# One filler job moved from the mLSTM heads to the attention, a third partial sum begun in the last head, and one weight sum fetched early in a hybrid mLSTM and sparse attention block

## The chip, the cores and the metric

The kernel runs on one core of one Trainium2 chip. The metric is device time in microseconds (us), lower is better: 615.52 us for the kernel before, the median of three runs (615.37, 615.52 and 616.9).

## The reference, cut to what matters

One decoder layer on 512 tokens of width 1024, in float32:

```
hN = rmsnorm(x, norm_g)
p  = split(hN @ w_in)                       # q, k, v, gates ... of both branches
mh = head_layernorm(mlstm(conv(q), conv(k), v, i, f))        # 4 heads of 256
ya = sigmoid(o) * mh * silu(z)
yb = nsa(...) * silu(z')                    # 8 heads of 64: compressed, selected, window
merged = sigmoid(g_a) * (ya @ w_branch_a) + sigmoid(g_b) * (yb @ w_branch_b)
x = x + merged @ w_out
out = rmsnorm(x, final_norm_g)
```

## The kernel before, in words

**Products.** Each float32 operand is split into a high part and a low rest (`split`, line 143: ScalarE or another engine rounds the high part, VectorE subtracts), and each block of a product is three matmuls: high by high, high by low, low by high. Weights come by `weights` (line 154): a DMA on SyncE's queue into a raw tile `wr`, then `wh` by ScalarE and `wl` by VectorE. Each of these three has three buffers, so a new DMA waits until VectorE has finished the split three loads back, and a new split waits until TensorE has finished the job three back.

**Filler.** Projections, gates and branch products are jobs of a queue, `Stream` (line 174). The attention and the mLSTM heads call `stream.step(n)` between their own matmuls; each step issues one filler matmul, and with no job left it issues nothing (lines 189 to 191). Loads run two jobs ahead. A gate job (`gate_ab`, line 575) is 24 matmuls of 512 columns, a tanh, and a store of its 256 KB to DRAM (`away`); there are sixteen, eight of `GB` and eight of `GA`, the latter in the order `in_turn` = 0, 4, 1, 5, 2, 6, 3, 7. Ten of them are queued before the attention (lines 782 to 797), six in the mLSTM's part (lines 1413 to 1416).

**Attention.** Sixteen units (line 1059). A unit computes the scores of the next unit, one call of `tick` (4 steps) after each of four, then transposes its own scaled probabilities `P` in four groups, again with a `tick` after each, and multiplies them with the values. The scaling of `P` by the reciprocal sum and the gate is four GpSimd operations behind the last score of a unit (lines 966 to 973). The last unit has no next one, so its scaling lies directly ahead of its own transposes. When the last head pair is collected, the path `zpath(3)` is added, 24 matmuls more.

**mLSTM heads.** Four heads, with 90 steps each: 24 between the scores, 24 between the value products, `NORM_FILL` = 30 behind the norm's small operations, and 6 behind each of the two groups of transposes that write `ya`. The queue there holds four convolution jobs, the gate jobs, eight jobs of branch B of 12 matmuls, and `first_of_a` (line 1396): the first six of eight blocks of branch A for two column groups, 18 matmuls each, which need only heads 0 to 2. Their sums stay open in PSUM, one in the bank `PO`, one in one of the three banks `PP`.

**Merge and end.** After the heads, `branch_a` (line 1541) finishes the eight column groups in the order `in_turn`: 6 matmuls where a sum is begun, 24 where none is. Behind each, VectorE multiplies with the gate `g`, adds branch B's part `b`, and splits the result; after each second group it forms four sums for the last product (`sums`, line 1529). That last product, by `w_out`, is done with seven half-size products in place of eight (a Strassen-Winograd scheme): four sums of blocks of `w_out` are made in DRAM by accumulating DMAs, in the chores of the heads (lines 1038 to 1049 and 1464), and loaded as weights. Each product is two jobs of 12 matmuls. The fourth sum is loaded by `load4` (line 1727) in two halves through `wr`, and split into the tiles `T4h` and `T4l` (`p4`). The last lines (`third`, `fourth`, `gen4`) form the final output rows, their norm and their stores, with the orders of ScalarE and VectorE fixed as written from `gen3` on (line 1751).

**Order.** The build orders each engine's instructions by their place in the program and by its own estimate of when their inputs are there; each engine then runs its list in order. Where the list has an instruction whose input is late, what stands behind it waits.

Of the kernel before, what the change touches and what calls it, by code (L numbers as in the profile page):

```python
# [11 lines left out]
F32 = mybir.dt.float32  # L12
F32R = mybir.dt.float32r
# [5 lines left out]
T = 512  # L19
# [57 lines left out]
def build(  # L77
# [3 lines left out]
    nc = tc.nc  # L81
# [24 lines left out]
    wp = ctx.enter_context(tc.tile_pool(name="wp", bufs=2))  # L106
    psum = ctx.enter_context(tc.tile_pool(name="psum", bufs=2, space=bass.MemoryType.PSUM))

    def bank(tag, bufs):
        return psum.tile([128, 512], F32, name=tag, tag=tag, bufs=bufs)  # L110

    PP = lambda: bank("pp", 3)
# [4 lines left out]
    def f(ap):  # L117
        return ap.bitcast(F32)
# [24 lines left out]
    def split(src, hi, lo, eng="a"):  # L143
        if eng == "a":
            A(hi, src, AF.Copy)
        elif eng == "p":
            pool.tensor_scalar(hi, src, 1.0, 1.0, OP.mult, OP.mult)
        else:
            dve.tensor_copy(hi, src)
        dve.tensor_tensor(lo, src, f(hi), OP.subtract)  # L150
# [3 lines left out]
    def weights(src, eng="a"):  # L154
        nk, n = src.shape[1], src.shape[2]
        raw = wp.tile([128, nk, n], F32, name="wr", tag="wr", bufs=3)
        nc.sync.dma_start(raw, src)
        hi = wp.tile([128, nk, n], F32R, name="wh", tag="wh", bufs=3)
        lo = wp.tile([128, nk, n], F32R, name="wl", tag="wl", bufs=3)
        split(raw, hi, lo, eng)  # L160
        return hi, lo
# [128 lines left out]
    with tc.tile_pool(name="ph0", bufs=2, side="right") as p0, tc.tile_pool(  # L290
        name="small", bufs=1, side="right"
# [3 lines left out]
        raw = sp.tile([128, ND, SW], F32, name="sraw")  # L295
# [279 lines left out]
    def gate_ab(base, j):  # L575
        def post(ps):
            s = stg.tile([128, T], F32, name="s", tag="s", bufs=2)
            A(s, ps, AF.Tanh, scale=0.5)
            away[base, j] = dram.tile([128, T], F32, name=f"away{base}_{j}")
            nc.sync.dma_start(away[base, j], s)  # L580

        cols(base + j * 128, post)

    in_turn = [j for i in range(4) for j in (i, i + 4)]
    gate_jobs = deque([(GB, j) for j in range(ND)] + [(GA, j) for j in in_turn])

    def gate_job(n=1):
        for _ in range(n):
            gate_ab(*gate_jobs.popleft())
# [3 lines left out]
    def conv(i, h, e):  # L593
        def post(ps):
            pl = cvp[-1]
            ct = h * 2 + e
            w = lambda j: prm[:, ct, i * 5 + j : i * 5 + j + 1]
            u = pl.tile([128, T], F32, name="u", tag="u", bufs=2)
            A(u, ps, AF.Identity, bias=w(4), scale=w(3))
            for s in (1, 2, 3):  # L600
                dve.scalar_tensor_tensor(u[:, s:], ps[:, : T - s], w(3 - s), u[:, s:], OP.mult, OP.add)
            th = pl.tile([128, T], F32, name="th", tag="th", bufs=1)
            A(th, u, AF.Tanh, scale=0.5)
            dve.scalar_tensor_tensor(u, th, 1.0, u, OP.add, OP.mult)
            both = pl.tile([128, 2, T], F32R, name="hl", tag="hl", bufs=2)
            split(u, both[:, 0], both[:, 1])
            if e == 0:
                qk[i, h] = dram.tile([128, 2, 2, T], F32, name=f"qk{i}{h}")
            nc.sync.dma_start(qk[i, h][:, :, e], f(both))

        cols((MQ, MK)[i] + (h * 2 + e) * 128, post)
# [3 lines left out]
    def conv_job(n=1):  # L615
        for _ in range(n):
            conv(*conv_jobs.popleft())
# [177 lines left out]
    for _ in range(3):  # L795
        gate_job()
        conv_job()


    def log_forget():  # L800
# [224 lines left out]
    wsum = {}  # L1025

    def begin_sum(w, n, src):
        wsum[w, n] = dram.tile([128, 4, 512], F32, name=f"wsum{w}{n}")
        tc.keep_in_program_order(nc.sync.dma_start(wsum[w, n], src))

    def add_to_sum(w, n, src):
        for q in range(2):
            part = slice(2 * q, 2 * q + 2)
            tc.keep_in_program_order(
                nc.gpsimd.dma_start(wsum[w, n][:, part], src[:, part], accum_op=OP.add)
            )

    def chores_of(w):
        (b11, b12), (b21, b22) = parts_of[w]
        return [  # L1040
            lambda: begin_sum(w, 1, b11),
            lambda: begin_sum(w, 3, b12),
            lambda: add_to_sum(w, 1, b12),
            lambda: begin_sum(w, 2, b22),
            lambda: add_to_sum(w, 3, b22),
            lambda: begin_sum(w, 4, b21),
            lambda: add_to_sum(w, 2, wsum[w, 1]),
            lambda: add_to_sum(w, 4, wsum[w, 2]),
        ]
# [8 lines left out]
    late, sums = deque(), {}  # L1058
# [53 lines left out]
    def ya(k):  # L1112
        return yah[:, k // 2, (k % 2) * T : (k % 2) * T + T]
# [282 lines left out]
    def first_of_a(j, bank):  # L1396
        def gen(w):
            ps = sums_a[j] = bank()
            for k in range(6):
                a, b, c, d = w[0][:, k], w[1][:, k], ya(k), yal[:, k]  # L1400
                pe.matmul(ps, a, c, start=k == 0, stop=False)
                yield
                pe.matmul(ps, a, d, start=False, stop=False)
                yield
                pe.matmul(ps, b, c, start=False, stop=False)
                if k < 5:
                    yield

        stream.add(lambda: weights(wav[:, :6, j * 128 : j * 128 + 128]), gen)
# [3 lines left out]
    for _ in range(4):  # L1413
        conv_job()
        gate_job()
    gate_job(2)
    for j in range(ND):
        branch_b(j)
    first_of_a(in_turn[0], PO)
    first_of_a(in_turn[1], PP)  # L1420
    chores.extend(chores_of("out"))

    decays = {}
# [20 lines left out]
    for h in range(4):  # L1444
# [5 lines left out]
        for sb in range(NT):  # L1450
            o, n = KOFF[sb], 512 - sb * 128
# [65 lines left out]
    with tc.tile_pool(name="fin", bufs=1) as fp:  # L1517
# [11 lines left out]
        def sums(i):  # L1529
            m, n = me.pop(i), me.pop(i + 4)  # L1530
            lo, hi = slice(0, 256), slice(256, 512)
            s12 = sgp.tile([128, T], F32, name="s", tag="s", bufs=AHEAD)
            s34 = sgp.tile([128, T], F32, name="s", tag="s", bufs=AHEAD)
            dve.tensor_tensor(s12[:, lo], n[:, hi], m[:, hi], OP.subtract)
            dve.scalar_tensor_tensor(s12[:, hi], s12[:, lo], -1.0, m[:, lo], OP.mult, OP.subtract)
            dve.tensor_tensor(s34[:, lo], m[:, lo], m[:, hi], OP.subtract)
            dve.scalar_tensor_tensor(s34[:, hi], s12[:, hi], -1.0, n[:, lo], OP.mult, OP.subtract)
            split(s12, hTh[:, 2 * i], hTl[:, 2 * i])
            split(s34, hTh[:, 2 * i + 1], hTl[:, 2 * i + 1])

        def branch_a(j):
            begun = j in sums_a
            k0 = 6 if begun else 0

            def load():
                g = fp.tile([128, T], F32, name="g", tag="g", bufs=6)
                nc.sync.dma_start(g, away[GA, j])
                b = fp.tile([128, T], F32, name="b", tag="b", bufs=3)
                nc.sync.dma_start(b, away["b", j])
                return weights(wav[:, k0:, j * 128 : j * 128 + 128]), g, b  # L1550

            def gen(held):
                w, t, b = held
                ps = sums_a[j] if begun else PP()
                for k in range(k0, ND):
                    p, q = w[0][:, k - k0], w[1][:, k - k0]
                    pe.matmul(ps, p, ya(k), start=k == 0, stop=False)  # L1557
                    yield
                    pe.matmul(ps, p, yal[:, k], start=False, stop=False)  # L1559
                    yield  # L1560
                    pe.matmul(ps, q, ya(k), start=False, stop=k == ND - 1)  # L1561
                    if k < ND - 1:
                        yield
                dve.scalar_tensor_tensor(t, t, 1.0, ps, OP.add, OP.mult)
                dve.tensor_tensor(t, t, b, OP.add)
                if j < 4:
                    split(t[:, :256], m11[0][:, j], m11[1][:, j])
                else:
                    split(t, mx2[0][:, j - 4], mx2[1][:, j - 4])
                me[j] = t  # L1570
                if j > 3:
                    sums(j - 4)

            stream.add(load, gen)

        for j in in_turn:
            branch_a(j)

# [143 lines left out]

        p3, p4, late = [], [], []

        def load4(q):
            if q == 0:
                p4.extend(fp.tile([128, 4, T], F32R, name=n) for n in ("T4h", "T4l"))
            ks = slice(2 * q, 2 * q + 2)  # L1730
            raw = wp.tile([128, 2, 512], F32, name="wr", tag="wr", bufs=3)
            nc.sync.dma_start(raw, wsum["out", 4][:, ks])
            split(raw, p4[0][:, ks], p4[1][:, ks])
            return [t[:, ks] for t in p4]

        def third(l):
# [82 lines left out]
```

## Time and profile before

| what | value |
|---|---|
| median of three runs | 615.52 us |
| profiled execution | 615.59 us, span of its instructions 613.8 us |
| granted TensorE clock | 0.996 of full speed |
| TensorE matmul busy | 600.3 us, 2985 matmuls |
| VectorE, ScalarE, GpSimd busy | 459.6, 357.4, 101.9 us |
| attention's last units | about 244 to 274.7 us in the span |
| mLSTM heads, to the last transposes | about 411 to 526.8 us |
| merge of the branches | 530.7 to 566.1 us |
| last product and end | 566.1 to 613.8 us |

PE is TensorE's matmul, PEld its weight load, DVE is VectorE, ACT ScalarE, POOL GpSimd, SPq the queue of SyncE. A row of the timeline gives start, duration, engine, line, operation and output<-inputs, and in brackets how long the engine had been idle before it and what ended that. A row of the windows gives a stretch, and for each engine its busy time and its instructions, then the granted clock, the busy share of the DMA engines and their rate in GB/s. Matmuls are pipelined: a matmul of 512 columns lasts 0.39 us in the rows, but the next one starts 0.23 us after it.

### The profile page before, as it was taken

The page shows a single profiled execution, that of the slowest core. Times are in us where ns is not written, and L with a number is a line of the kernel's source. Part 1 is how long each engine was busy: PE and PEld are TensorE (multiplying, and loading weights), DVE is VectorE, ACT ScalarE, POOL GpSimd, SP SyncE. Part 2 cuts the span into 40 slices and gives each one's busy share as a digit, 9 for nine tenths or more (in the row PEclk, how much of TensorE's full clock was granted, in tenths as well). Part 3 has the DMA queues.
Part 4 walks back from the last instruction along what each step waited for, and adds up shares of the span by engine and source line. Part 5 has one row for each costly group of instructions (what it writes and reads, how often), then busy time and mean ns, then how long its engine had stood idle before and what let it go on. Part 6 is the DMA issues. An engine that isn't in the chain of part 4 may idle for free.

```text
span 613.8 us, 8697 instructions
## 1 busy us (share of the span) xinstructions
PE 600.3 (98%) x2985; PEld 498.9 (81%) x2985; DVE 459.6 (75%) x870; ACT 357.4 (58%) x667; POOL 101.9 (17%) x183
## 2 busy tenths in 40 slices
PE   8999999999999999999999999999999999999994
PEld 6988888878887877868888888888888888888873
DVE  4876767898878787669989655688767666588785
ACT  5765646656676576556756665456646453353554
POOL 6220002324232225330000000000202110000013
PEclk9999999999999999999999999999999999999998
DMA  8546865757694766577775466797999895993753
GB/s 285 165 126 164 225 211 160 155 171 173 166 260 119 178 204 138 149 168 222 238 248 169 132 195 194 217 312 242 312 337 224 311 208 178 291 312 127 274 171 137
DMA packets 104155, 126.87 MB, mean 207 GB/s; under 512 B 5120, under 2 KB 65700, under 8 KB 104112
## 3 DMA queue, kind: packets, MB, share of 16 engines
q1 hardware_dynamic: 98542, 112.69, 58.1%
q0 software_dynamic: 4992, 12.58, 13.0%
q10 hardware_dynamic: 578, 1.05, 0.5%
q8 instruction: 23, 0.38, 0.2%
q14 instruction: 20, 0.16, 0.1%
HBM read 108.48 MB, written 41.94 MB: 245 GB/s over the span
## 4 chain that ended last, share of the span: by engine, by line
PE 48%; DMA 3%; DVE 2%; ACT 1%; issue 1%; POOL 1%; SPq 0%; ACTq 0%; POOLq 0%
PE pp L214 6%; PE pp L216 6%; PE pp L212 5%; PE pp L1240 3%; PE pp L1242 3%; PE pp L1244 3%; PE pp L1561 2%; PE pp L1557 2%; PE pp L1559 2%; PE pt L1242 2%; PE pt L1244 2%; PE pt L1240 2%; DMA wr<-w_out 2%; PE ps L1240 1%; PE ps L1242 1%; PE ps L1244 1%
## 5 line engine op out<-in xcount | busy, mean ns | idle before, releaser
L92 DVE TENSOR_TENSOR wl<-wr,wh 128x1024 fp32r<-128x1024 f32 (+2 forms) x104 | 126.4, 1217 | 55.8 <-ACT wh L92 50.6
L92 ACT ACTIVATE wh<-wr 128x1024 fp32r<-128x1024 f32 (+2 forms) x104 | 108.1, 1041 | 59.2 <-PE pp L214 12.0
L212 PE MATMUL pp<-hTh,wh 128*128 128x512 f32 (+1 forms) x360 | 141.5, 393 | 0.0
L214 PE MATMUL pp<-hTl,wh 128*128 128x512 f32 (+1 forms) x360 | 141.1, 392 | 0.0
L216 PE MATMUL pp<-hTh,wl 128*128 128x512 f32 (+1 forms) x360 | 141.0, 392 | 0.0
L216 PEld LDWEIGHTS pp<-hTh,wl 128*128 128x128 f32 x360 | 67.9, 189 | 11.4
L212 PEld LDWEIGHTS pp<-hTh,wh 128*128 128x128 f32 x360 | 67.9, 189 | 10.9
L214 PEld LDWEIGHTS pp<-hTl,wh 128*128 128x128 f32 x360 | 68.0, 189 | 10.7
L92 POOL TENSOR_SCALAR P<-P,st,gates 128x128 f32<-128x128 f32 (+1 forms) x64 | 47.7, 758 | 171.7 <-DVE st L92 144.7
L92 ACT ACTIVATE P<-P,st 128x128 f32<-128x128 f32 (+3 forms) x64 | 35.7, 558 | 34.5 <-DVE st L92 34.1
L92 DVE CUSTOM_DVE_ANT_0 P<-ps,cst 128x128 f32<-128x128 f32 (+3 forms) x64 | 30.2, 483 | 14.4 <-PE ps L963 13.1
L92 POOL TENSOR_TENSOR rlr<-va,mhalf 128x4 f32<-128x4 f32 x4 | 4.2, 1038 | 215.2 <-DVE va L92 215.2
L92 ACT ACTIVATE pth<-pt 128x512 fp32r<-128x512 f32 (+1 forms) x64 | 27.0, 433 | 21.8 <-PE pt L979 15.8
L92 DVE TENSOR_TENSOR ptl<-pt,pth 128x512 fp32r<-128x512 f32 (+1 forms) x64 | 29.9, 481 | 11.3 <-ACT pth L92 11.1
L92 DVE SCALAR_TENSOR_TENSOR u<-pp,prm,u 128x511 f32<-128x511 f32 (+2 forms) x48 | 35.5, 739 | 0.3
L979 PE MATMUL pt<-cst,P 128*128 128x128 f32 x160 | 28.9, 277 | 1.7 <-POOL P L92 1.0
L979 PEld LDWEIGHTS pt<-cst,P 128*128 128x128 f32 x160 | 20.2, 141 | 12.6 <-DVE ptl L92 5.9
L92 ACT ACTIVATE th<-u 128x512 f32<-128x512 f32 x16 | 10.1, 630 | 20.4 <-DVE u L92 17.5
L992 PE MATMUL po<-ptl,vsw 128*128 128x512 f32 (+1 forms) x64 | 21.2, 332 | 0.0
L991 PE MATMUL po<-pth,vsw 128*128 128x512 f32 (+1 forms) x64 | 20.6, 322 | 0.3 <-ACT pth L92 0.3
L1561 PE MATMUL pp<-yah,wl 128*128 128x512 f32 x50 | 19.5, 389 | 0.0
L1557 PE MATMUL pp<-yah,wh 128*128 128x512 f32 x50 | 19.5, 389 | 0.0
(411 smaller groups left out, 1353.2 us busy)
## 6 DMA issues: line engine op xcount, KB each, us to landing
wr<-w_in SPq DMA_DIRECT2D x68, 512.0 KB, 4.1
qk<-hl SPq DMA_DIRECT2D x16, 512.0 KB, 5.7
qk<-qk SPq DMA_DIRECT2D x16, 512.0 KB, 7.7
away<-s SPq DMA_DIRECT2D x16, 256.0 KB, 3.4
wsumv<-w_in SPq DMA_DIRECT2D x4, 1024.0 KB, 6.4
wsumz<-w_in SPq DMA_DIRECT2D x4, 1024.0 KB, 6.3
wr<-wsumv SPq DMA_DIRECT2D x8, 512.0 KB, 4.6
wr<-wsumz SPq DMA_DIRECT2D x8, 512.0 KB, 3.7
```

Of the source, the lines that this page charges most:

```text
L92: ins = fn(*args, **kw)
L212: pe.matmul(ps, a, c, start=k == 0, stop=False)
L214: pe.matmul(ps, a, d, start=False, stop=False)
L216: pe.matmul(ps, b, c, start=False, stop=k == nk - 1)
L979: pe.transpose(pt[:, (qb - kb) * 128 : (qb - kb) * 128 + 128], P[:, POFF[qb] + kb * 128 : POFF[qb] + kb * 128 + 128], ident,)
L991: pe.matmul(po[:, kb * 128 :], vl, th[:, :n], start=b == 0 and kb == 0, stop=False)
L992: pe.matmul(po[:, kb * 128 :], vl, tl[:, :n], start=False, stop=False)
L1240: pe.matmul(ps, a, c, start=begin, stop=False, skip_group_check=not first)
L1242: pe.matmul(ps, a, d, start=False, stop=False, skip_group_check=not first)
L1244: pe.matmul(ps, b, c, start=False, stop=k == 3, skip_group_check=not first)
L1557: pe.matmul(ps, p, ya(k), start=k == 0, stop=False)
L1561: pe.matmul(ps, q, ya(k), start=False, stop=k == ND - 1)
```

## The change

The eleventh gate job goes from the mLSTM's queue to the end of the attention's. `first_of_a` is added for a third column group, in a bank `PP`. The fourth sum of `w_out` is no longer loaded in two halves through `wr`: one DMA of 1 MB, placed in the load of the seventh column group of branch A between that group's `b` and its weights, writes it into `T4l`, which is allocated ahead of branch A. `load4` then splits it in place: ScalarE writes `T4h` from `T4l`, and VectorE overwrites `T4l` with the difference.

```diff
@@ before the attention
     for _ in range(3):
         gate_job()
         conv_job()
+    gate_job()
@@ the mLSTM's queue
-    gate_job(2)
+    gate_job()
     for j in range(ND):
         branch_b(j)
     first_of_a(in_turn[0], PO)
     first_of_a(in_turn[1], PP)
+    first_of_a(in_turn[2], PP)
@@ branch_a, load
                 nc.sync.dma_start(b, away["b", j])
+                if j == in_turn[6]:
+                    nc.sync.dma_start(f(p4[1]), wsum["out", 4])
                 return weights(wav[:, k0:, j * 128 : j * 128 + 128]), g, b
@@
+        p4 = [fp.tile([128, 4, T], F32R, name=n) for n in ("T4h", "T4l")]
         for j in in_turn:
             branch_a(j)
@@
-        p3, p4, late = [], [], []
+        p3, late = [], []
 
         def load4(q):
-            if q == 0:
-                p4.extend(fp.tile([128, 4, T], F32R, name=n) for n in ("T4h", "T4l"))
             ks = slice(2 * q, 2 * q + 2)
-            raw = wp.tile([128, 2, 512], F32, name="wr", tag="wr", bufs=3)
-            nc.sync.dma_start(raw, wsum["out", 4][:, ks])
-            split(raw, p4[0][:, ks], p4[1][:, ks])
+            split(f(p4[1][:, ks]), p4[0][:, ks], p4[1][:, ks])
             return [t[:, ks] for t in p4]
```

## The prediction, made before the run

> **What bounds the kernel.** I read the page's first part, then the waits of TensorE, then the windows and timelines of the three places that the change touches.
>
> ```profile
> PE 600.3 (98%) x2985; PEld 498.9 (81%) x2985; DVE 459.6 (75%) x870; ACT 357.4 (58%) x667; POOL 101.9 (17%) x183
> ```
>
> ```profile
> PE pt L979 <- POOL P L92: 1.0, 2, 0.6
> PE pp L1678 <- DVE T4l L92: 0.6, 2, 0.4
> ```
>
> TensorE is busy for 600.3 us of the span of 613.8, and the change takes away no matmul: it moves 24 of a gate job and 18 of branch A. So it can gain only where TensorE waits, or behind its last matmul. The list of waits names both targets: transposes of `P` behind GpSimd, and the last product behind VectorE's `T4l`. The rate of TensorE comes from a stretch without a wait, two jobs of the last product.
>
> ```profile
> 571.51 0.39 PE L1677 MATMUL pt<-wh,hTh 128*128 128x512 f32 x1
> 576.95 0.39 PE L1677 MATMUL pp<-wh,hTh 128*128 128x512 f32 x1
> ```
>
> Between these starts lie 24 matmuls: 5.44 us, 0.227 us each. A wait is therefore best measured from start to start, less 0.227 us for a matmul of 512 columns.
>
> **Part 1, the gate job in the attention.** From the code: before, the queue of jobs runs dry behind the third `tick` of the scores in unit 14, and the last 13 ticks find no job. The moved job adds 24 steps, which fill six of them: the one behind the last unit's last score, the four between unit 14's transposes, and the first one of unit 15. All of these lie between the last score and the first transposes of unit 15, where `P` is scaled.
>
> ```profile
> 252.00:260.00 8.00, 8.00 (x41) 6.47 (x40) 6.47 (x13) 4.90 (x10) 4.97 (x6) 1.00 0.45 103
> 260.00:264.00 4.00, 3.69 (x21) 2.82 (x21) 3.35 (x7) 3.56 (x7) 0.00 (x0) 1.00 1.03 211
> 264.00:268.00 4.00, 3.85 (x20) 2.91 (x20) 3.80 (x9) 2.03 (x6) 2.22 (x3) 1.00 0.35 113
> 268.00:272.00 4.00, 3.16 (x17) 2.20 (x18) 1.42 (x4) 1.47 (x3) 2.70 (x4) 1.00 0.74 151
> ```
>
> ```profile
> 263.12 0.39 PE L214 MATMUL pp<-hTl,wh 128*128 128x512 f32 x1
> 263.82 0.50 PE L991 MATMUL po<-pth,vsw 128*128 128x512 f32 x1 [0.31 <-ACT pth L92]
> 265.78 3.33 POOL L92 TENSOR_SCALAR P<-P,st,gates 128x128 f32<-128x128 f32 x4 [8.54 <-PE pt L979]
> 267.44 0.41 PE L979 MATMUL pt<-cst,P 128*128 128x128 f32 x2
> 268.42 0.33 PE L979 MATMUL pt<-cst,P 128*128 128x128 f32 x1 [0.57 <-POOL P L92]
> 269.17 0.33 PE L979 MATMUL pt<-cst,P 128*128 128x128 f32 x1 [0.42 <-POOL P L92]
> ```
>
> The columns of a window are PE, PEld, DVE, ACT and POOL. TensorE's idle time by its busy time is 0.31 + 0.15 + 0.84 = 1.30 us from 260 to 272, and none from 252 to 260. From start to start it is more: 263.12 to 263.82 is 0.70 us in place of 0.23, and from 267.44 to 269.17, 1.73 us, go three transposes, for which the four of the row at 526.17 below (0.35 us to the next matmul) give 0.26 us. That is 0.47 + 1.47 = 1.9 us. The cover added is 24 x 0.227 = 5.44 us, more than the waits, even if the moved job's split on VectorE (1.22 us in the group's row below, with VectorE at 3.80 of 4 us from 264 to 268) delays the last softmax by its whole length. The bounds are 0 (the engine's list puts the matmuls elsewhere and the waits stay) and 1.9; I take 1.8, near the count by starts, since the matmul behind a wait is itself longer (0.50 against 0.39). The job's own 5.44 us are no cost: they leave the later part.
>
> [...]
>
> **Part 2, the third early sum.** In the heads' queue the steps are 4 x 90 = 360. Before, 10 x 24 + 8 x 12 + 2 x 18 = 372 are wanted, so 12 are left behind the last transposes; after, 9 x 24 + 96 + 3 x 18 = 366, so 6 are left.
>
> ```profile
> 526.17 0.60 PE L1503 MATMUL pt<-cst,num 128*128 128x128 f32 x4
> 526.52 0.47 PE L1401 MATMUL pp<-yah,wh 128*128 128x512 f32 x1
> 527.53 0.75 DVE L92 SCALAR_TENSOR_TENSOR yal<-pt,prm,yah 128x512 fp32r<-128x512 f32 x1 [0.52 <-ACT yah L92]
> 530.71 0.39 PE L1557 MATMUL po<-yah,wh 128*128 128x512 f32 x1
> ```
>
> The merge now starts 6 x 0.227 = 1.36 us sooner, at 529.35, and its last input is there at 528.28 (527.53 + 0.75): 1.1 us to spare, no wait. It has 3 x 6 + 5 x 24 = 138 matmuls in place of 156, so it ends 1.36 + 4.08 = 5.44 us sooner, at 560.6 against 566.07, which is what part 1 has paid. TensorE comes out even. VectorE doesn't: the same results now come in less time.
>
> ```profile
> 531.00:566.00 35.00, 29.53 (x47) 1.00 0.80 250
> 540.00:545.00 5.00, 4.92 (x8) 1.00 1.12 326
> ```
>
> ```profile
> L92 DVE TENSOR_TENSOR wl<-wr,wh 128x1024 fp32r<-128x1024 f32 x8 | 9.8, 1220 | 4.7 <-PE po L1557 3.5 <-ACT wh L92 1.2
> ```
>
> These windows are VectorE's alone: 29.53 of 35 us (84%) in the merge. After the change the third group's weights there are a quarter as large, about 0.9 us less: 28.6 us of work. The first result is ready 6 matmuls behind 529.35, at 530.7, so there are 29.9 us: 96%. From 540 to 545 VectorE already ran at 4.92 of 5 with TensorE unbroken, so at best nothing is late. At 92% the work takes 31.1 us, 1.2 late. Lateness isn't absorbed, as the place behind the merge shows:
>
> ```profile
> 572.86 0.69 DVE L92 TENSOR_TENSOR hTl<-s,hTh 128x512 fp32r<-128x512 f32 x1 [0.36 <-ACT hTh L92]
> 573.58 0.33 SPq L1586 DMA_DIRECT2D s<-x  x1
> 574.07 1.38 SPq L157 DMA_DIRECT2D wr<-w_out  x2
> 580.27 1.06 ACT L92 ACTIVATE wh<-wr 128x1024 fp32r<-128x1024 f32 x1 [4.73 <-DMA wr<-w_out]
> 582.64 0.19 PEld L1678 LDWEIGHTS ps<-wl,mx 128*128 128x128 f32 x1 [0.29 <-DVE wl L92]
> ```
>
> VectorE's last rest `hTl` frees a buffer, only then SyncE's queue issues the last load of `x` and, behind it, two quarters of `w_out`; ScalarE waits for them, and TensorE has a wait of 0.29 us already. A delay of VectorE goes through this chain to TensorE in full. Between 0 and 1.2 us I take 0.6.
>
> [...]
>
> **Part 3, the fourth sum.** Two DMAs of 512 KB and two places in `wr` go from the end; one DMA of 1 MB comes earlier.
>
> ```profile
> 588.71 2.83 SPq L1732 DMA_DIRECT2D wr<-wsumout  x2
> 595.77 1.22 DVE L92 TENSOR_TENSOR T4l<-wr,T4h 128x1024 fp32r<-128x1024 f32 x1
> 595.92 1.06 ACT L92 ACTIVATE T4h<-wr 128x1024 fp32r<-128x1024 f32 x1 [0.79 <-DMA wr<-wsumout]
> 596.38 0.39 PE L1677 MATMUL pt<-wh,hTh 128*128 128x512 f32 x1
> 597.04 0.50 PE L1678 MATMUL pp<-T4l,mx 128*128 128x512 f32 x1 [0.27 <-DVE T4l L92]
> 598.23 1.22 DVE L92 TENSOR_TENSOR T4l<-wr,T4h 128x1024 fp32r<-128x1024 f32 x1
> 598.76 0.39 PE L1679 MATMUL pt<-wh,hTl 128*128 128x512 f32 x1
> 599.50 0.50 PE L1678 MATMUL pp<-T4l,mx 128*128 128x512 f32 x1 [0.35 <-DVE T4l L92]
> ```
>
> By starts, TensorE loses 0.66 - 0.23 = 0.43 us at 596.38 and 0.74 - 0.23 = 0.51 us at 598.76: 0.94 us. With the data loaded in the merge, both subtractions can be done before, and third and fourth product run through. Behind the last matmul a little more may go:
>
> ```profile
> 605.60 0.28 PE L1679 MATMUL pp<-T4h,mx 128*128 128x256 f32 x1
> 606.17 0.16 DVE L92 TENSOR_TENSOR li<-lf 128x1 f32<-128x1 f32 x1 [1.26 <-ACT po L92]
> 606.43 0.42 DVE L92 SCALAR_TENSOR_TENSOR g<-pp,s 128x256 f32<-128x256 f32 x1
> ```
>
> TensorE ends at 605.88, but VectorE reads its result at 606.43, 0.55 us later, behind a small operation that waited for ScalarE's squares; those come sooner without the two splits of `T4h` among them. Bounds: 0 (the chain of the norm sets the end) and 0.94 + 0.55 = 1.5; I take 1.2, the whole wait and half of the rest. The new DMA costs SyncE's queue one issue; `T4l` is free from the start of the merge and the accumulating DMAs ran in the last head, so it should hold up nothing in that queue but the weights right behind it. At the 326 GB/s of 540 to 545, where the DMA engines are full (1.12), 1.05 MB delay those by 3.2 us; they are fetched two jobs ahead, 10.9 us, which covers this and their split. The split in place is the same two operations. If the cover fails, the 3.2 us stand against the gain.
>
> **The sum**, against the profiled execution's 615.59 us: 615.59 - 1.8 - 1.2 + 0.6 = 613.2. It stands 0.07 above the median of 615.52, so I predict 613.1. The bounds: all gains and no cost, 615.59 - 1.9 - 1.5 = 612.2.
>
> **The rivals.**
> *The waits for `P` stay.* The lists are made at build time by estimates; already before, matmuls were put ahead of their place (those of line 214 at 263.12 can only be `zpath(3)`'s, as the queue was dry) and two waits stood nevertheless. If the gate's matmuls go ahead of the last scores, part 1 gives 0: 615.0. Against it: in program order they lie behind that score. Chance 0.22.
> *The end isn't TensorE's.* If the norm's small chain sets the end whatever TensorE does, part 3 gives 0: 614.4. The 0.55 us above speak for it, the waits on `T4l` against it. Chance 0.10.
> *VectorE becomes the bound of the merge*, the slower case. If it keeps its 84%, 28.6 us of work take 34.0, 4.1 us late: 615.59 - 3.0 + 4.1 = 616.7. With the two subtractions of `T4l` put into this stage (2.4 us more), 31.0 / 0.84 = 36.9, 7.0 late: 619.6. It decides from a lateness of 3.0 us on, that is a pace below 87%, or 94% with `T4l`. Its cause would be what made VectorE's gaps before, ScalarE's half of each split and late DMAs. Against it stands the 98% window. Chance 0.12.
>
> **The numbers.** The forecast has the remaining 0.56, within 612.2 and 614.0. About 0.3%, 1.85 us, is what a measurement of this kernel tells from no change, so faster means under 613.67; 0.06 of the forecast's share lies above that. Of the slower rival's 0.12, 0.02 lie within 0.3% (its lower price, 616.7, does). Faster 0.50, same 0.06 + 0.22 + 0.10 + 0.02 = 0.40, slower 0.10. The range goes from 612.0 to 616.7, where the slower rival begins.
>
> **What would show it.** Right: no wait of transposes for `P` at the end of the attention and none for `T4l`; the merge with 138 matmuls and no gap; VectorE above 92% there; TensorE's last matmul some 2.4 us sooner. Wrong: gaps at the first products of `w_out` with ScalarE or VectorE as the releaser, a DMA of `T4l` that holds SyncE's queue, or transposes still behind GpSimd.

## The result, and the profile after

| | median | range | runs |
|---|---|---|---|
| before | 616.03 us | 615.03 to 617.37 | 22 |
| after | 619.86 us | 616.11 to 626.15 | 22 |

The changed kernel takes 1.0061 times as long as the one before, with a 95% interval of 1.0041 to 1.008: slower by 0.6%, where 0.4% faster was forecast. Its times also scatter more: 616.11 to 624.26 us, 8 us in place of 2.3, and one run by itself at 626.15, the slowest, which the ratio leaves out. The profiled execution took 620.04 us, with a span of 618.2 us and a granted clock of 0.992 (before 615.59, 613.8 and 0.996).

First the page's line of busy times and the list of TensorE's waits of the changed kernel (waited for, total, times, longest):

```profile
PE 602.4 (97%) x2985; PEld 500.6 (81%) x2985; DVE 458.4 (74%) x871; ACT 356.7 (58%) x668; POOL 101.8 (16%) x183
```

```profile
PE ps L170 <- DVE Dm L92: 2.1, 1, 2.1
PE ps L1682 <- ACT wh L92: 1.3, 1, 1.3
PE ps L1683 <- DVE wl L92: 0.8, 1, 0.8
```

The work is the same, and the two waits that the change aimed at, for `P` and for `T4l`, are gone. Three others have come: one in the mLSTM's scores (line 170), two in the last product.

Where the time went is counted from start to start: for each pair of neighbouring matmuls the distance, less the usual distance of such a pair, summed over a stretch. This gives 4.5 us before and 2.6 after for the attention's end (250 to 275 us in the span), 0.5 and 4.5 for head 1 (440 to 460), 0.2 and 4.3 for the first half of the last product (580 to 592), 1.3 and 0.1 behind that. With 0.8 us less in the first 30 us and 0.1 more elsewhere the sum is 4.3 of the 4.4 us between the spans.

**The two gains.** The window of the attention's end, and from the timeline the last scaling of `P` and the end of the kernel:

```profile
262.00:274.00 12.00, 11.88 (x66) 9.29 (x64) 8.10 (x15) 6.61 (x14) 3.88 (x6) 1.00 0.89 214
```

```profile
264.20 2.37 POOL L92 TENSOR_SCALAR P<-P,st,gates 128x128 f32<-128x128 f32 x4 [7.45 <-DVE st L92]
...
610.26 0.28 PE L1684 MATMUL pp<-T4h,mx 128*128 128x256 f32 x1
...
610.58 0.42 DVE L92 SCALAR_TENSOR_TENSOR g<-pp,s 128x256 f32<-128x256 f32 x1
```

TensorE is idle for 0.12 of 12 us (before, 1.30), and `P` is scaled from 264.20 to 266.57 beside the moved job's matmuls. At the end it waits for nothing, and VectorE reads the last result 0.04 us after the last matmul (610.54 to 610.58), not 0.55.

**The loss in head 1.** The third load of `w_in` behind head 0, on each engine in turn (in the kernel before, the first row's issue took 0.50 us, at 439.03):

```profile
442.12 4.97 SPq L157 DMA_DIRECT2D wr<-w_in  x1
...
450.62 1.06 ACT L92 ACTIVATE wh<-wr 128x1024 fp32r<-128x1024 f32 x1 [3.06 <-DMA wr<-w_in]
...
451.71 1.23 DVE L92 TENSOR_TENSOR wl<-wr,wh 128x1024 fp32r<-128x1024 f32 x1 [3.42 <-ACT wh L92]
452.86 0.88 DVE L92 SCALAR_TENSOR_TENSOR Dm<-ps,Dm 128x384 f32<-128x384 f32 x2
...
450.93 0.40 PE L216 MATMUL pp<-hTh,wl 128*128 128x512 f32 x1
453.46 0.33 PE L170 MATMUL ps<-qk,qk 128*128 128x128 f32 x1 [2.14 <-DVE Dm L92]
```

The issue takes 4.97 us, the data is there 8.5 us after its start (before 5.98), and VectorE's list has the split `wl` of these weights ahead of the scores' scaling `Dm`, which frees the bank for the next scores. So weights that TensorE doesn't need yet stop it for 2.3 us.

**The loss in the last product.** The chain that the prediction priced, and what follows the wait:

```profile
551.54 1.22 DVE L92 TENSOR_TENSOR T4l<-T4l,T4h 128x1024 fp32r<-128x1024 f32 x1
...
557.55 1.22 DVE L92 TENSOR_TENSOR T4l<-T4l,T4h 128x1024 fp32r<-128x1024 f32 x1
...
575.08 1.47 DVE L92 TENSOR_TENSOR hTl<-s,hTh 128x512 fp32r<-128x512 f32 x2
...
573.17 4.66 SPq L1591 DMA_DIRECT2D s<-x  x5
578.43 1.10 SPq L157 DMA_DIRECT2D wr<-w_out  x2
...
584.57 1.06 ACT L92 ACTIVATE wh<-wr 128x1024 fp32r<-128x1024 f32 x1 [5.96 <-DMA wr<-w_out]
...
585.65 1.23 DVE L92 TENSOR_TENSOR wl<-wr,wh 128x1024 fp32r<-128x1024 f32 x1 [4.42 <-ACT wh L92]
...
583.98 0.39 PE L1684 MATMUL pp<-wh,hTl 128*128 128x512 f32 x1
585.67 0.51 PE L1682 MATMUL ps<-wh,mx 128*128 128x512 f32 x1 [1.31 <-ACT wh L92]
586.93 0.51 PE L1683 MATMUL ps<-wl,mx 128*128 128x512 f32 x1 [0.76 <-DVE wl L92]
```

VectorE does both subtractions of `T4l` in the middle of the merge. Its last `hTl` ends 8.7 us behind the merge's end at 567.88 (before 7.5 behind 566.07), the issue of `w_out` comes 10.55 us behind it (before 8.0), and TensorE stops for 1.47 and 1.03 us, start to start.

Both stalls cost more than the wait. Windows behind the last product's and behind head 1's:

```profile
587.60:591.00 3.40, 3.40 (x10) 2.65 (x9) 2.75 (x3) 0.81 (x1) 0.00 (x0) 0.50 0.64 183
454.40:457.80 3.40, 3.40 (x11) 2.78 (x11) 0.98 (x4) 0.66 (x2) 0.00 (x0) 0.51 0.94 283
```

For 3.4 us the granted clock is one half, and 512 columns take 0.43 us in place of 0.23: 1.4 to 1.7 us more each time. When a wait was followed by this in the traces stands in the last section.

### The profile page after: what moved, and what is told of

The parts are those of the page before. It is cut to its first block, busy times and chain, and to the rows that moved or that the text cites. A ratio compares the mean times of both kernels' runs of the same rounds, so it can differ in the third digit from the quotient of the medians.

```text
span 618.2 us, 8701 instructions
## 1 busy us (share of the span) xinstructions
PE 602.4 (97%) x2985; PEld 500.6 (81%) x2985; DVE 458.4 (74%) x871; ACT 356.7 (58%) x668; POOL 101.8 (16%) x183
## 4 chain that ended last, share of the span: by engine, by line
PE 76%; DVE 11%; DMA 7%; ACT 3%; issue 2%; SPq 0%; POOL 0%; POOLq 0%; ACTq 0%; DVEq 0%
PE pp L212 12%; PE pp L214 12%; PE pp L216 12%; PE pp L1241 3%; PE pp L1243 3%; PE pp L1245 3%; DMA wr<-w_in 2%; PE pt L980 2%; DVE wl L92 2%; PE pt L1243 2%; PE pt L1241 2%; PE pt L1245 2%; PE pp L420 2%; DVE u L92 2%; ACT wh L92 1%
## 5 line engine op out<-in xcount | busy, mean ns | idle before, releaser
L1243 PE MATMUL pp<-wl,S 128*128 128x512 f32 x48 | 18.7, 389 | 0.0
L1245 PE MATMUL pp<-wh,S 128*128 128x512 f32 x48 | 18.7, 389 | 0.0
```

The source lines that it names most:

```text
L1243: pe.matmul(ps, a, d, start=False, stop=False, skip_group_check=not first)
L1245: pe.matmul(ps, b, c, start=False, stop=k == 3, skip_group_check=not first)
```

## The experiments

All medians, of 12 runs each (4 or 5 for e10 to e12), with the kernel before on the same chip. Its medians there were 615.75 to 616.8 us. Its own times scatter over 3.2 us on the chip of e1 to e4 and 3.9 on that of e17 and e18, but over 6 to 7 us on those of e5 to e16, so a range of 5 or 6 us there says little by itself.

| run | median, range us | ratio to before, 95% |
|---|---|---|
| e1 changed kernel again | 620.33, 615.1 to 624.2 | 1.0064, 1.0041 to 1.0088 |
| e2 gate job and third sum | 618.04, 614.2 to 621.5 | 1.0039, 1.0016 to 1.0062 |
| e3 fourth sum early | 617.66, 614.0 to 622.1 | 1.0021, 0.9998 to 1.0044 |
| e4 gate job | 619.04, 613.9 to 620.9 | 1.0038, 1.0016 to 1.0059 |
| e5 sums from head 1 on | 619.99, 617.0 to 622.4 | 1.0044, 1.002 to 1.0068 |
| e6 changed, `T4l` split behind | 617.99, 616.0 to 622.5 | 1.0021, 0.9998 to 1.0044 |
| e7 as e3, `T4l` split behind | 616.81, 615.2 to 619.5 | 1.0002, 0.9978 to 1.0025 |
| e8 e5 and e6 together | 618.79, 617.3 to 621.8 | 1.0041, 1.0022 to 1.006 |
| e9 as e3, `T4l` split between | 614.68, 613.4 to 615.8 | 0.9965, 0.9945 to 0.9984 |
| e10 changed, sums in the strips | 631.54, 629.7 to 631.8 | 1.024, 1.0205 to 1.0275 |
| e11 e10 and split between | 627.08, 626.6 to 628.6 | 1.018, 1.0146 to 1.0215 |
| e12 before, sums in the strips | 629.84, 629.1 to 632.2 | 1.0228, 1.0195 to 1.0262 |
| e13 changed, split between | 616.45, 614.0 to 619.8 | 1.0003, 0.9983 to 1.0023 |
| e14 e13, copies in the attention | 617.07, 615.4 to 620.0 | 1.0008, 0.9987 to 1.0029 |
| e15 e9, copies in the attention | 617.63, 615.8 to 620.3 | 1.0023, 1.0005 to 1.004 |
| e16 e14 without the third sum | 616.84, 615.4 to 620.9 | 1.0004, 0.9978 to 1.003 |
| e17 e14, last adds in place | 617.08, 613.1 to 619.8 | 1.0008, 0.9986 to 1.003 |
| e18 e16, last adds in place | 614.09, 612.9 to 616.5 | 0.9972, 0.9957 to 0.9986 |

### Which part makes which stall (e1 to e4)

e1 is the changed kernel, unaltered. e2 takes part 3 back, e3 and e4 put one part alone into the kernel before:

```diff
@@ e3: part 3 alone
+                if j == in_turn[6]:
+                    nc.sync.dma_start(f(p4[1]), wsum["out", 4])
...
+            split(f(p4[1][:, ks]), p4[0][:, ks], p4[1][:, ks])
@@ e4: the gate job alone
+    gate_job()
...
-    gate_job(2)
+    gate_job()
@@ e2: e4 and the third sum
+    first_of_a(in_turn[2], PP)
```

> The changed kernel once more. Its first trace has two stalls that the kernel before does not have: 4.2 us in the scores of head 1 (a wait of 2.3 us, then matmuls at half pace) and 3.95 us in the last product at 584 to 591 us (waits of 1.47 and 1.03 us, then half pace). Theory A (late transfers in the merge stall the last product) expects the second stall in this profile again, within 1 us of its size. Theory B (the stall in head 1 hangs on a transfer that is sometimes late) expects the first stall to be there or not, and the times to scatter over 616 to 626 us as before. If both are accidents of one execution, this profile shows neither and the time is near 614.

> Gate job moved and third early sum, but the fourth sum of w_out is loaded late, as before. Theory A1 (the shorter merge leaves VectorE and the chain behind it too little time): the stall of 3.95 us in the last product stays, and the two waits for T4l of 0.94 us are back, so about 620.8 us if head 1 stalls too, 616.6 if not. Theory A2 (the 1 MB transfer in the middle of the merge delays the loads behind it): no stall in the last product, 0.94 us for T4l, so 615.3 without a stall in head 1 and 619.5 with it.

> Only the early load of the fourth sum, in the long merge of the kernel before (156 matmuls). A1: no stall, the gain of 0.9 us at the end, 615.1 us. A2: the 1 MB transfer delays the loads behind it here as well, so a stall of 1 to 4 us in the last product, 616 to 619 us. Theory B, if the stall in head 1 comes from the moved gate job: no stall there and a scatter as small as before's, about 2 us.

> Only the gate job moved; the heads' queue then runs dry 12 steps before its end, so the merge starts sooner in the order of work and has its 156 matmuls as before. The waits for P at the end of the attention go (1.7 us), the dry steps cost up to 12 x 0.227 = 2.7 us behind the last norm. If the stall in head 1 comes from the moved job (B), it is here too: about 621 us with it, 616 to 617 without, and the times scatter over more than 5 us. No stall in the last product by A1 (the merge is as long as before) and by A2 (no early 1 MB transfer).

Both stalls repeat in e1 (2.5 us waited in head 1, 0.9 and 0.8 us in the last product). The waits of e2, of e3 and of e4, in this order:

```profile
PE ps L170 <- DVE Dm L92: 2.2, 1, 2.2
PE pp L1680 <- DVE T4l L92: 0.7, 1, 0.7
PE ps L1680 <- DVE wl L92: 0.6, 1, 0.6
```

```profile
PE ps L1680 <- ACT wh L92: 0.8, 1, 0.8
PE ps L1681 <- DVE wl L92: 0.8, 1, 0.8
```

```profile
PE ps L170 <- DVE Dm L92: 1.4, 1, 1.4
PE pp L1679 <- DVE T4l L92: 0.7, 1, 0.7
```

They come apart cleanly. The wait of head 1 is in all four traces with the moved job (after, e1, e2, e4) and not in e3; start to start it costs 1.9 to 4.2 us, of which the half clock is a part in the changed kernel's trace alone. The large stall of the last product, 3.6 to 4.1 us of which 1.5 to 1.6 are the half clock, is there where `T4l` is loaded early (after, e1, e3). In e2, with the shorter merge alone, it is 0.8 us, and in e4 nothing. So A1 holds for 0.8 us, about what part 2 was priced at; the rest is part 3's, which makes the stall by itself in e3, and B is the gate job's. The scatter is in all three part kernels (7 to 8 us, where the kernel before has 3.2 on this chip): neither stall alone makes it.

### Is it the transfer or the subtractions? (e6, e7, e9)

The early `T4l` brings a transfer of 1 MB and two subtractions into the merge. In e6 (the changed kernel) and e7 (e3) the transfer stays, and the lists of ScalarE and VectorE are made to have the splits behind the weights of the fifth product:

```diff
+        def pinned(load):
+            def run(q):
+                ordered.update(("act", "dve"))
...
+        product(stiles(2), pinned(from_sums(3)), Y, False, after7)
...
+            stream.add(lambda q=q: pinned(load4)(q) if q else pinned(load4)(q) and None, gen4)
```

> The changed kernel, where the fourth sum is loaded into T4l in the merge as before, but ScalarE's and VectorE's lists have its two splits behind the fifth product's weights, where they stood in the kernel before. Theory A2 (the 1 MB transfer in the merge delays what is loaded behind it): the stall of 3.8 us in the last product stays, about 620. Theory A3 (the two subtractions, 1.22 us each, take VectorE's time in the merge, and all of its later work, the last load of x and w_out behind it come later): the stall falls to about 0.8 us as in the run without part 3, about 617, and there is no wait for T4l at the end.

> The kernel before with part 3 alone, the splits of T4l held behind as in the run above: the 1 MB transfer lies in the long merge of 156 matmuls, and VectorE's list is that of the kernel before. A2: a stall of 3.8 us in the last product as with part 3 alone, 617.9 in the profile. A3: no stall there, the gain of 0.9 us at the end, 615.0 in the median, and a scatter as small as before's 3 us.

In e7 the stall is gone: the issue of `w_out` stands 7.96 us behind the merge's end, as in the kernel before (8.0; e3: 9.9), with the transfer still in the merge. In e6 it is 1.0 us (3.8 in e1), near e2's. That is A3; A2 falls. e3's trace alone would not show it: there VectorE also waited 3.05 us at 541 us for the `wh` of a late load of `w_branch_a` (before 1.20, e7 1.6), and e15 below, with the splits behind, has the issue of `w_out` 1.3 us late after a wait of 3.5 us at the same load. But the time of e7 was 1.8 us above what was expected: ScalarE's `T4h` now stood behind two squares of the norm, and TensorE waited 0.7 us for it; and head 1 had a wait of 1.1 us although no job was moved. e9 puts both splits right behind those of the fifth product:

```diff
+        def fifth(q):
+            ordered.update(("act", "dve"))
+            w = from_sums(3)(q)
+            if q:
+                for i in range(2):
+                    ks = slice(2 * i, 2 * i + 2)
+                    split(f(p4[1][:, ks]), p4[0][:, ks], p4[1][:, ks])
+            ordered.clear()
+            return w
```

> The kernel before with part 3 alone, and the splits of T4l now held right behind those of the fifth product's weights, in both lists ahead of the squares (in the last run of this kind ScalarE's T4h stood behind two squares, and TensorE waited 0.7 us for it). Theory A3: no stall in the last product, no wait for T4l or T4h, so the gain of 0.9 us of part 3 is seen: 616.0 - 0.9 = 615.1 in the median. If the 1 MB transfer itself costs something in the merge: 616 or more, with a wait behind a load there.

e9's list of waits has none at the end and none in the last product:

```profile
PE pt L979 <- POOL P L92: 1.0, 2, 0.6
PE ps L170 <- DVE Dm L92: 0.7, 1, 0.7
```

The gain of part 3 is now seen: 614.68 us, 0.35% under the kernel before (interval 0.16 to 0.55%, that is 1.0 to 3.4 us, so if anything more than the 0.9 us expected), with a scatter of 2.4 us. The same two splits cost 0.56% in the middle of the merge (e3 against e9), and 0.61% in the changed kernel (e1 against e13 below).

### What stops head 1? (e5, e8, e10 to e12)

e5 deals the chores of the heads out anew; e8 adds e6's edit:

```diff
-        for _ in range(2):
+        for _ in range((0, 3, 3, 2)[h]):
             chores.popleft()()
```

> The changed kernel with the chores of the heads dealt out as 0, 3, 3, 2 in place of 2, 2, 2, 2: in head 0 no block of w_out is copied for a weight sum and none is added. In all three profiles with the moved gate job the third load of w_in behind head 0 is issued at the same place, but the issue takes 4 to 5 us in place of 0.5 and the data lands 2.5 us later, and VectorE's list has its split ahead of the scores' scaling in head 1. Theory B1 (the weight sums' transfers in head 0 fill the DMA engines, and the load had no slack): the stall of 1.6 to 4.2 us in head 1 goes, the median falls from 620 to 616 to 617, with the stall in the last product of 3.8 us still there. Theory B2 (the stall comes from the missing job itself, by the order of the lists): the stall stays, 620.

> The changed kernel with both edits, chores dealt out 0, 3, 3, 2 and the splits of T4l behind. A3 and B1 together: no stall in head 1, 0.8 us or less in the last product, the gains of 1.7 us in the attention and 0.9 us at the end, so 616.0 - 2.6 + 0.8 = 614.2, faster than both kernels. A2 with B1: about 617. B2 with A3: 617 to 618.

The scores of head 1 have no wait in either; the third load's issue takes 0.38 us in both. But there is a new wait. e5's list, and two rows of its timeline:

```profile
PE pt L1505 <- DVE num L92: 1.6, 1, 1.6
PE ps L1682 <- ACT wh L92: 1.5, 1, 1.5
PE ps L1683 <- DVE wl L92: 0.8, 1, 0.8
```

```profile
465.45 2.37 POOL L1036 DMA_DIRECT2D wsumout<-w_out  x2 [29.75 <-DMA wsumout<-w_out]
468.92 0.17 DVE L92 TENSOR_TENSOR rlt<-va,rlr 128x4 f32<-128x4 f32 x1 [4.09 <-POOL rlr L92]
```

The transposes of `num` are at 470 us, 19 us later, and this is not the old stall in another place, as the expectation of e10 below has it: GpSimd's list has the issue of the adds, which waits for the copies, ahead of the reciprocal root `rlr` of the norm, and VectorE waits 4.09 us for the root (in the changed kernel 1.2). It is a fault of this way to deal out the chores, so the medians of e5 and e8 say nothing against B1. There is another wait, of 0.2 us, at 512. e8 has both as well (0.7 and 0.4 us), and 0.6 us each for `wl` and `T4h` in the last product. Its expected 614.2 us missed by 4.6. e10 to e12 take the sums out of the heads altogether, into the 42 strip jobs; e11 has e9's edit as well, e12 is the kernel before:

```diff
-    stream.run(6 * 7)
+    chores.extend(chores_of("out"))
+    for _ in range(8):
+        stream.run(5)
+        chores.popleft()()
+    stream.run(2)
```

> The changed kernel, with all chores of w_out (four copies of 1 MB and eight added halves) moved out of the heads into the 42 strip jobs between attention and heads, where the DMA engines are busy for 0.44 to 0.84. Theory B1 (the sums' transfers take the load of w_in its slack; dealt out later they only moved the stall to head 2): no stall in any head, the scatter falls to before's, and with the stall in the last product left 616.0 - 2.6 + 3.8 = 617.2. Theory B2 (missing job): stall of 2 to 4 us in head 1 as before, about 620. If the strips have no room either: waits of TensorE for wl between 290 and 400 us.

> The changed kernel with both edits, sums formed in the strips and the splits of T4l behind those of the fifth product's weights. A3 with B1: the attention's 1.7 us and the end's 0.9 us are gained and 0.8 us or less lost in the last product: 616.0 - 2.6 + 0.8 = 614.2 or a little less, faster than the kernel before. With B2: 617 to 618. If the scatter has another cause than the sums, the median lies 2 to 3 us above the profiled execution, as in the runs so far.

> The kernel before, only the chores of w_out moved from the heads into the strip jobs. B1: its heads had just enough slack (one execution of a kernel with before's heads showed a wait of 1.1 us at the same place), so the median stays at 616.0 or falls by up to 1 us and the scatter is smaller. If the strips have no room: slower than 616.5, with waits between 290 and 400 us.

There the sums cost far more, 11 to 15 us in the medians. e10's list:

```profile
PE pp L1241 <- ACT wh L92: 3.5, 2, 1.9
PE pp L1243 <- DVE wl L92: 2.8, 4, 0.8
...
PE ps L1683 <- ACT wh L92: 1.9, 1, 1.9
PE ps L1684 <- DVE wl L92: 0.8, 1, 0.8
```

Lines 1241 and 1243 are the strips; in the three traces TensorE loses 13 to 17 us between 290 and 400 us. That a share of the DMA engines of 0.44 to 0.84 (in the kernel before, from 270 to 390 us) left no room for the copies and adds is the author's guess, which no other run tests. The heads, with the moved job and without the sums, have no wait at their scores in e10 and e11: B1 holds there, B2 falls.

### The copies or the adds? (e13 to e18)

e13 is the changed kernel with e9's edit. In e14 to e18 the four copies that begin the sums are issued in the attention, and the adds stay in the heads, in GpSimd's list behind the root; e14 to e16 pop one pair of adds in each head, e17 and e18 as shown:

```diff
+        if i in (3, 6, 10, 13):
+            out_chores[(0, 1, 3, 5)[(3, 6, 10, 13).index(i)]]()
...
-        for _ in range(2):
-            chores.popleft()()
...
         r = rsqrt(mp, va, NT, "rl")
+        for _ in range((1, 1, 2, 0)[h]):
+            chores.popleft()()
```

> The changed kernel with the splits of T4l right behind those of the fifth product's weights, nothing else. Left are the gains of 1.7 and 0.9 us, part 2's price in the last product (0.8 to 1.0 us) and head 1's stall (1.6 to 4.2 us in the traces with the moved job): 616.0 - 2.6 + 0.9 + 1.6 to 4.2 = 615.9 to 618.5, and a scatter of over 5 us. If the stall in head 1 were only of the profiled executions, 614.3.

> As e13, and the four 1 MB copies that begin the sums of w_out are issued in units 3, 6, 10 and 13 of the attention; the added halves stay in the heads, each pair behind the reciprocal root of its head, where they ran before. Theory B1 (the load behind head 0 has no slack against 2 MB of copies and the adds): no stall in head 1, 614 to 614.5, scatter of 3 us or less. If the adds alone are enough to delay the load (their stretch has 160 to 210 GB/s in all traces): the stall stays at 1 us or more. If the attention has no room for 4 MB more: waits for wl between 100 and 240 us.

> Part 3 alone with the splits of T4l behind the fifth product's (e9, 614.7), and the copies in the attention as in e14. B1: the wait of 0.7 us in head 1 that e9's profile has goes, 614.0; if the attention pays for the copies, 615 or more.

> As e14 without the third early sum: the heads' queue runs dry 12 steps before its end (0.5 us more behind the last norm in the run with the gate job alone), but the merge has its 156 matmuls and VectorE its time. B1 and part 2's price of 0.8 us in the last product: 616.0 - 2.6 + 0.5 = 613.9, as fast as e14 or faster.

e13's profiled execution took 613.96 us and had no wait in head 1, though the job is moved; its median was 616.45. So with the same code for the heads this stall is there in one execution and not in another. With the copies away the load's issue is short in every trace. The queue in e14, then in e13:

```profile
442.30 0.38 SPq L157 DMA_DIRECT2D wr<-w_in  x1
```

```profile
442.85 1.56 SPq L157 DMA_DIRECT2D wr<-w_in  x1
```

The third load's issue in the traces, beside TensorE's wait at the scores of head 1:

| kernel | issue us | wait us |
|---|---|---|
| job not moved: before, e3, e9, e7 | 0.50, 0.53, 2.94, 2.93 | 0, 0, 0.7, 1.1 |
| job moved: e13, e6, e4, e1, after, e2 | 1.56, 4.21, 4.25, 4.78, 4.97, 5.06 | 0, 1.4, 1.4, 2.5, 2.1, 2.2 |
| copies not in head 0: e5, e8, e14, e16, e17, e18 (job moved), e15 (not moved) | 0.38 each | 0 |

So this load is held only where the two copies are ahead of it in SyncE's queue, and the kernel before too was on the edge. The adds alone don't hold it: in e14 they are issued 7.1 us ahead of the load (in the changed kernel 4.2), and their packets run from 437.1 to 448.2 us, all through the load's issue. Whether the copies hold it by themselves isn't separated: in the changed kernel the adds' packets begin 5.0 us after their issue (in e14 1.9), at 442.9 us, 0.8 us into the load's issue, and no run has the copies without the adds. But e14 to e16 had a fault of their own, against what was expected of them: the last pair of adds ran at 522 us, not at 498 to 509. e14 then waited 2.8 us for `wl` in the merge, and e14 to e16 1.3 to 2.1 us in the last product (e14 2.1, e16 1.7). Their times, 616.8 to 617.6, say nothing for or against the copies' place.

> As e14, with the adds dealt out 1, 1, 2, 0 behind the roots of the heads, so that the last pair runs from about 497 us as in the changed kernel, not from 522. If that pair made the waits for wl in the merge (2.5 us at 537, 0.6 us at 556): they go, and with no wait in head 1 the profiled execution is at 614 to 614.5, the median within 1.5 us of it. If the copies in the attention shift the merge's loads in another way: the waits stay and the time is 617 as for e14.

> The same without the third early sum. Part 2's price (waits for wh and wl in the last product, 1.7 us in the trace of e13) should be absent, as it was with the gate job alone, and 0.5 us more waits behind the last norm: 613 to 613.5 in the profiled execution. If the waits in the last product are there without the third sum as well (e16 had 2.1 us of them), they come from the loads, not from the shorter merge.

With the pair back in its place the waits for `wl` in the merge are gone from e18, and e17 has 0.15 us left of them. From the lists of e18 and then of e17:

```profile
PE ps L1688 <- DVE wl L92: 0.8, 1, 0.8
...
PE ps L1687 <- ACT wh L92: 0.3, 1, 0.3
```

```profile
PE pt L1478 <- ACT num L92: 1.5, 1, 1.5
PE ps L1689 <- DVE wl L92: 0.7, 1, 0.7
```

e18, the gate job moved, the fourth sum early and no third sum, is faster than the kernel before by 0.28%, about as much as e9 (both intervals overlap). In its trace the attention's gain of 1.8 us and the end's of 1.2 are both there, and the waits of the last product take 1.4 us back. e17, with the third sum too, isn't: on the same chip its median is 3.0 us higher. Its profiled execution took 617.45 us in place of the expected 614 to 614.5. It shows one new wait in the heads, at 518 us in the last one, where VectorE waited 4.96 us for `b`, a load of branch B; start to start TensorE loses 1.5 us more there than in e18, but 1.9 us more in the first 30 us, where both kernels are the same. So what the third sum costs isn't settled: 3.0 us in the medians of e17 against e18, 0.2 in e14 against e16, and a gain of 1.0 in e2 against e4. And the waits of the last product are in e18 without the third sum, so they aren't its price alone.

## Why the prediction was wrong, point by point

Of the 6.8 us between the 613.2 us of the sum and the 620.04 of the profiled execution, 4.0 lie in head 1, for which the sum had no term, and 3.5 in the last product; 0.8 us came off in the first 30 us, where both kernels are the same.

- **Part 1, gain of 1.8 us: right.** The attention's end lost 1.9 us less, start to start, and the waits for `P` went. The rival that they stay falls.
- **"The job's own 5.44 us are no cost: they leave the later part": this failed.** The sum had no term for the heads. With the job gone from their queue, the issue of a load that had no slack took 4.2 to 5.1 us in five of six traces (in the changed kernel's its data came 2.5 us later), and TensorE lost 4.0 us in the profiled execution of the changed kernel. The gate job alone makes the kernel 0.38% slower (e4). The prediction followed the 24 matmuls and not the queue of transfers that they were moved out of, with 2 MB of copies and the adds in it. That the load is held only behind the copies is shown (e5, e8, e14, e16 to e18); why the moved job makes its issue longer is not, and stays open.
- **Part 2, cost of 0.6 us: right in one trace, not settled by the medians.** In e2, `w_out` is issued 8.67 us behind the merge's end in place of 8.0, and TensorE loses 0.8 us. But e18 has such waits without the third sum, and the medians give no one price (above). That at best nothing is late at 96% was the prediction's own conclusion from one window of 5 us at 98%, and such a share doesn't tell it: in e2 VectorE is busy for 27.51 of the merge's last 30 us, 92%, and late.
- **Part 3, gain of 1.2 us: right.** 0.9 us at the two waits, and from the last matmul's end to the span's end 7.66 us in place of 7.92: 1.1 to 1.2 us.
- **"The split in place is the same two operations": this is the other step that failed.** The same two, but the lists put them into the merge, ahead of work that the last product waits for. The issue of `w_out` comes 0.67 us later with the shorter merge alone (e2), 1.92 with the early fourth sum alone (e3) and 2.55 with both. How busy VectorE is doesn't tell this: in the merge's last 30 us it is busy for 28.33 in the changed kernel, 25.31 before and 25.38 in e3 (in this order):

```profile
538.00:568.00 30.00, 28.33 (x46) 1.00 0.89 296
```

```profile
536.00:566.00 30.00, 25.31 (x42) 1.00 0.76 234
```

```profile
536.00:566.00 30.00, 25.38 (x43) 1.00 0.86 275
```

- The price of 2.4 us was in the prediction, but in the rival only. The 1 MB transfer, on which the forecast spent its caution, made TensorE wait for nothing in the merge in e7 and e9.
- **"A delay goes through this chain to TensorE in full": too little.** `w_out` was issued 2.55 us later, the waits were 2.50 us, and the half clock behind them added 1.4.
- **The rival *VectorE becomes the bound of the merge*** was what happened in the last product: its chain, its place, and about its lower price (4.1 us named, 3.95 lost between 580 and 590 us). That the two figures agree is luck: 1.4 us of the loss are the half clock, and the lateness itself was 2.55 us. Its sign, gaps at the first products of `w_out`, is in the trace; no sign had named head 1. It got 0.12, since a window at 98% had shown TensorE unbroken. But inside the merge nothing waits for VectorE; its lateness is paid 16 us later, in the last product, and there was the 0.29 us of wait that should have said that the chain has no slack.

## What to carry to other kernels

An operation that is moved earlier can cost time on its engine at the new place, even when its inputs and the consumer allow it (here two subtractions of 1.22 us each in the merge, and in e3 the issue of `w_out` 1.92 us later): ask for the busiest engine there what is late at the end of that stage. A load that lands just in time has no slack for what is ahead of it in its queue (the third load of `w_in` behind head 0: an issue of 0.38 us without the two copies ahead of it, up to 5.06 us with them), and where an engine's list has its split ahead of urgent work, the whole chain stops for data that nobody needs yet (2.3 us at the scores of head 1). When a change widens the scatter (here from 2.3 to 8 us), look for such loads in several traces, not in one, and know first how much the kernel before scatters on that chip (3.2 to 7 us on the chips of the experiments).

## What the runs showed of the hardware

**In these traces the half clock followed a wait or not by where the wait lay in a grid of 3.41 us.** The changed kernel's waits of 1.47 and 1.03 us are followed by 3.4 us at a granted clock of 0.50. e14 has the same two waits and then runs on at full clock:

```profile
585.04 0.49 PE L1687 MATMUL ps<-wh,mx 128*128 128x512 f32 x1 [1.30 <-ACT wh L92]
586.30 0.50 PE L1688 MATMUL ps<-wl,mx 128*128 128x512 f32 x1 [0.77 <-DVE wl L92]
```

```profile
586.00:590.00 4.00, 3.69 (x16) 3.08 (x17) 3.72 (x5) 1.29 (x2) 0.00 (x0) 1.00 0.56 139
```

Within each of the 20 traces the stretches at half clock begin whole multiples of 3.413 us apart: in the changed kernel at 454.50, 587.62 and, behind the last matmul, 614.92 us, that is 39.0 and 8.0 such steps. Laid over the matmuls behind the first 35 us, this grid sorts the waits of these traces without exception: each cell of it at full clock in which TensorE lost 2.03 us or more, counted start to start, is followed by half clock (13 cells in 8 traces), and none in which it lost 1.91 us or less. In e14 the border of a cell at 585.67 us cuts the two waits, so that the first cell holds 1.86 us; e1's wait in head 1, 2.71 us and longer than the changed kernel's 2.30, is cut at 452.50 into 1.21 and 1.50 and isn't followed by half clock.

**A DMA issue on SyncE's queue itself took 0.38 to 5.06 us,** for the same 512 KB load at the same place: 0.38 without the two copies ahead of it, 0.50 to 5.06 with them (the table of e13). While the adds into DRAM ran behind head 0, from 440 to 446 us in the kernel before and from 443 to 449 in the changed one, the 16 DMA engines were busy (a mean share of 1.00 to 1.13 in windows of 2 us), but moved 184 to 211 GB/s. Shortly before, from 428 to 434 and from 431 to 435 us, they moved 395 to 406 GB/s at a share of 1.00 to 1.06.
